# A recurrent unit's last tile in token halves, and the order of the output projection's last products

## The chip, the cores and the metric

The kernel runs on one NeuronCore of a Trainium2 chip, as one program. What counts is the device time of a run in microseconds; the figure of a kernel is the median of its runs. A profiled execution gives the trace; times in it are microseconds from the start of its span. Engines: PE is TensorE (matmuls; its weight loads are PEld), DVE is VectorE, ACT is ScalarE, POOL is GpSimd, and SP mostly issues DMAs.

## The reference, cut to what matters

One inference step of two trunk layers with 1024 features. 512 latent tokens (a grid of 8 rows by 64 columns) and 128 prompt tokens go through layer 0 (attention) and layer 1 (a recurrent unit), each followed by a SwiGLU network. The change lies in layer 1, between its recurrent unit and its output projection:

```python
def _linear_scan(a, b, h0, reverse):
    def step(h, ab):
        a_t, b_t = ab
        h = a_t * h + b_t
        return h, h
...
    b = jnp.sqrt(-jnp.expm1(2.0 * log_a)) * (i * xc)
...
    hs_f, hT_f = _linear_scan(a_f, b_f, h0[:, 0], reverse=False)
    hs_b, hT_b = _linear_scan(a_b, b_b, h0[:, 1], reverse=True)
    y = (hs_f + hs_b).astype(xm.dtype) * jax.nn.gelu(gate)
    return y @ w_out, jnp.stack([hT_f, hT_b], axis=1)
...
        lat = lat + g1_l[:, None, :] * o_l
```

Latent and prompt tokens are scanned apart from each other, each forward and backward; the final states of the prompt scans are an output. All is float32.

## The kernel before, in words

Features lie on the 128 partitions, in eight tiles of 128 (`KT`), tokens along the free axis: columns 0 to 511 latent, 512 to 639 prompt. The two halves of the tokens, `CH`, are columns 0 to 319 and 320 to 639, so the second half holds the last 192 latent columns and all prompt columns. A float32 product is made of three passes: each operand is split into a high part, rounded by a cast to the matmul type (float32r; `whi` or `yhi`), and a low part, the rest (`wlo`, `ylo`); a chunk's 24 matmuls are high x high, high x low and low x high over eight k-tiles. `unit` (L164) loads a weight by SP into one of three `raw` buffers and splits it: cast on ACT, subtraction on DVE (L183). In the recurrent unit's own stage the cast is a DMA of POOL instead (L179).

The recurrent unit is a software pipeline over feature tiles (L1473 to L1487). `lru_a` makes the gates, `lru_b` (L1310) the decay `a` and the input `ti`, whose last two steps are a square root on ACT (L1321) and its product on DVE (L1322) over both directions at once, 2 x 643 columns. `lru_c` (L1325) scans in place on DVE, per direction 512 latent and 128 prompt columns, copies the end states to `st` (L1332), and adds the two directions, the latent ones in two pieces that also turn rows of the grid into columns (L1337), then the prompt ones (L1338). `lru_d` (L1341) multiplies by the gate `G` (L1343) and splits the result into `yhi` (ACT) and `ylo` (DVE); for the last tile it does so in the two token halves. The write of `st` to memory follows on POOL's queue (L1488).

The output projection `project_halves` (L1036) has eight output tiles f. The weights of f = 0 to 2 are ready early. Five chunks, both halves of f = 0 and 1 and the first half of f = 2, are held open in five PSUM banks: three of tag `mm`, two of `mx`, whose third bank is free. They take the k-tiles 0 to 4 in a loop, and the last three k-tiles together, since those come out of the recurrent unit late:

```python
        for k in range(KT - 3, KT):
            if k == KT - 1:
                self.keep(self.ps("at"), 10)
            for (f, t0, t1), ps in turns:
```

`keep` (L207) issues small float32 matmuls that only keep TensorE at work. Ahead of the last k-tile there are ten. When a chunk ends, `out` (L1037) adds it on DVE into `x` (`residual`, L598), squares it on ACT, and writes it to memory by SP. `x` is loaded whole from memory, four DMAs on SP's queue (L1371), into a buffer in the space that the recurrent unit's tiles leave. Then come f = 3 to 7 for the first half, with weights loaded into buffers as they come free, and f = 2 to 7 for the second.

Order: the program is traced in the order of the source, and a scheduler then orders each engine's instructions by its own estimate of the time, so independent work may go ahead of what stands before it. `pin(ins)`, or `issue_after(ins)`, says that an instruction goes behind `ins` on its engine. A tile placed where another lay waits for that one's last reader.

Of the kernel before, what the change touches and what calls it, by code (L numbers as in the profile page):

```python
# [9 lines left out]
F32 = mybir.dt.float32  # L10
F32R = mybir.dt.float32r
AF = mybir.ActivationFunctionType
ALU = mybir.AluOpType
# [4 lines left out]
KT = D // P  # L18
NLAT = 512
NTOK = 640  # L20
# [5 lines left out]
ROWS = 8  # L26
# [8 lines left out]
LW = 643  # L35
NLT = 10
C0 = 515
FG = (1, 1, 1)
MODS = ((0, 2), (0, 4), (0, 3), (0, 5), (1, 1), (1, 0), (1, 4), (1, 3), (1, 2), (1, 5))
# [87 lines left out]
class _Step:  # L127
# [35 lines left out]

    def unit(self, src, slot=None, after=None, nx=3):  # L164
        nc = self.nc
        _, a, b = src.shape
        raw = self.t([P, a, b], F32, "raw", 3)
        nc.sync.dma_start(raw, src)
        if slot is None:
            self.nu += 1  # L170
            slot = "x" if self.wx and self.nu % 2 == 0 else "m"
        if slot == "x":
            hi = self.t([P, a, b], F32R, "whx", nx, self.sb)
            lo = self.t([P, a, b], F32R, "wlx", nx, self.sb)
        else:
            hi = self.t([P, a, b], F32R, "whi", 3)
            lo = self.t([P, a, b], F32R, "wlo", 3)
        if self.ptags == ["at"]:
            nc.gpsimd.dma_start(hi, src)  # L179
        else:  # L180
            nc.scalar.copy(hi, raw)  # L181
        with self.tc.issue_after(after) if after else nullcontext():
            nc.vector.tensor_tensor(lo, raw, hi.bitcast(F32), ALU.subtract)  # L183
        return hi, lo
# [850 lines left out]

    def project_halves(self, w, hi, lo, gk, key, xd):  # L1036
        def out(f, t0, t1, ps):  # L1037
# [6 lines left out]
        for (f, t0, t1), ps in zip(early, pss):  # L1044
            self.some(us[f], hi, lo, t0, t1, ps, range(KT - 3))
        turns = sorted(zip(early, pss), key=lambda e: e[0][1])
        for k in range(KT - 3, KT):
            if k == KT - 1:
                self.keep(self.ps("at"), 10)
            for (f, t0, t1), ps in turns:  # L1050
                for part in us[f]:
                    self.done = self.nc.tensor.matmul(ps, part[:, k], hi[:, k, t0:t1], start=False, stop=False).ins
            for (f, t0, t1), ps in turns:
                self.done = self.nc.tensor.matmul(ps, us[f][0][:, k], lo[:, k, t0:t1], start=False, stop=(k == KT - 1)).ins
                if k == KT - 1:
                    out(f, t0, t1, ps)
        for f in range(3, KT):
            us.append(self.unit(w[f], "mx"[f % 2]))
            out(f, *CH[0], self.chunk(us[f], hi, lo, *CH[0]))
        self.rt = self.t([P, NTOK], F32, "r", 2)  # L1060
# [249 lines left out]
    def lru_b(self, f, lt, tr, ti):  # L1310
# [7 lines left out]
        for d in range(2):  # L1318
            p2 = self.sp2[:, d * KT + f:d * KT + f + 1]
            self.turn(AF.Exp, lambda: nc.scalar.activation(tr[:, d], tr[:, d], AF.Tanh, scale=p2, bias=p2))  # L1320
        self.turn(AF.Sqrt, lambda: nc.scalar.activation(tr, tr, AF.Sqrt, scale=0.25))  # L1321
        nc.vector.tensor_tensor(ti, ti, tr, ALU.mult)  # L1322
        return a, ti

    def lru_c(self, f, a, h):  # L1325
        nc = self.nc
        for d in range(2):
            for sl, init in ((slice(0, NLAT), self.col(f"h{d}", f)), (slice(C0, LW), 0.0)):
                hv, av = [t[:, d, sl] if d == 0 else t[:, d, sl][:, ::-1] for t in (h, a)]
                nc.vector.tensor_tensor_scan(hv, av, hv, init, ALU.mult, ALU.add)  # L1330
        ends = bass.AP(tensor=h.tensor, offset=h[:, 0, LW - 1:LW].offset, ap=[list(h.ap[0]), [C0 + 1, 2]])
        nc.vector.tensor_copy(self.st.rearrange("p (d k) -> p k d", d=2)[:, f], ends)  # L1332
        y = a[:, 0, 0:NTOK]
        fn, bn = [h[:, d, 0:NLAT].rearrange("p (r c) -> p c r", r=ROWS) for d in range(2)]
        for c0, c1, q0 in ((56, 64, 0), (0, 56, 64)):
            yv = y[:, q0:q0 + (c1 - c0) * ROWS].rearrange("p (c r) -> p c r", r=ROWS)
            nc.vector.tensor_tensor(yv, fn[:, c0:c1], bn[:, c0:c1], ALU.add)  # L1337
        nc.vector.tensor_tensor(y[:, NLAT:NTOK], h[:, 0, C0:LW], h[:, 1, C0:LW], ALU.add)  # L1338
        return y

    def lru_d(self, f, y, G, yhi, ylo):  # L1341
        for a, b in CH if f == KT - 1 else ((0, NTOK),):
            self.nc.vector.tensor_tensor(y[:, a:b], y[:, a:b], G[:, a:b], ALU.mult)  # L1343
            self.split(yhi[:, f, a:b], ylo[:, f, a:b], y[:, a:b])

# [27 lines left out]
    def run(self):  # L1373
# [83 lines left out]
        with self.phase("lru", at=1) as lp:  # L1457
# [15 lines left out]
            for t in range(KT + 2):  # L1473
# [5 lines left out]
                if 0 < t <= KT:  # L1479
                    B[t - 1] = self.lru_b(t - 1, *A.pop(t - 1))  # L1480
                if t > 1:
                    C[t - 2] = self.lru_c(t - 2, *B.pop(t - 2))
                for g in {KT - 1: (KT - 3, KT - 2), KT: (KT - 1,)}.get(t, (t - 2,)):
                    for step in gate(g) if 0 < g < KT - 1 + (t == KT) else ():
                        step()
                if t > 1:
                    self.lru_d(t - 2, C.pop(t - 2), G.pop(t - 2), yhi, ylo)  # L1487
            nc.gpsimd.dma_start(o["nh"], self.st)  # L1488
        x1, x2 = self.big(n=PITCH), self.big(n=PITCH)
        self.new_x(self.ctx)  # L1490
        self.load_x(xd)
        with self.phase("ffn1", at=1, mx=3, mc=1, wx=2) as fp:
# [4 lines left out]
            self.X["B12h"], self.X["B12l"] = self.X["T4h"], self.X["T4l"]  # L1497
            self.project_halves(i["wlo"], yhi, ylo, (1, 2), (1, 1), xd)
            self.hhi, self.hlo = self.big(n=PITCH), self.big(n=PITCH)
# [23 lines left out]
```

## Time and profile before

| | us |
|---|---|
| median of 3 runs | 1506.66 |
| lowest and highest | 1506.61, 1507.72 |
| the profiled execution's own time | 1508.43 |
| its span in the trace | 1506.4 |
| PE busy in it | 1483.1 |

The own time of the profiled execution is 2.0 us above its span, for what lies around the span. The trace lists instructions with start and duration. A duration of DVE or ACT holds the way through the engine, so that the next instruction may start a little ahead of its end; where it needs the result it starts behind it. Matmuls overlap likewise: their distance from start to start is the cost. In square brackets stands idle time of the engine ahead of an instruction, and what ended it. Chip time 1003 to 1025 is the stretch around the change.

### The profile page before, as it was taken

How to read it: one execution, taken by the hardware profiler on the slowest of the kernel's cores; microseconds unless marked ns; L12 is line 12 of the kernel's file. 1: busy time of each engine (PE TensorE's matmuls, PEld its weight loads, DVE VectorE, ACT ScalarE, POOL GpSimd, SP SyncE). 2: the span in 40 equal slices, each digit the busy share in tenths (PEclk: the TensorE clock that was granted, in tenths of full speed). 3: DMA queues.
4: the chain of work that ended last, by engine and by line, in shares of the span. 5: the costliest groups of instructions: out<-in, count | busy, mean ns of one | idle time of the engine just before them, and what ended most of it. 6: DMA issues, size and time to landing. Idle time of an engine off the chain costs nothing. (4 is left out here: it accounts for less than half of the span.)

```text
span 1506.4 us, 26172 instructions
## 1 busy us (share of the span) xinstructions
PE 1483.1 (98%) x10409; PEld 1435.1 (95%) x10409; DVE 1063.1 (71%) x2015; ACT 701.6 (47%) x1271; POOL 222.5 (15%) x260
## 2 busy tenths in 40 slices
PE   8999999999999999999999999999999999999997
PEld 6999999899999999999999988899999999999997
DVE  5778998679999997444443778986975665655555
ACT  4576766664332123312321569884634342524243
POOL 0112132101111110000000100000331323232311
PEclk9999999999999999999999999999999999999999
DMA  9644766446566664222222544325233131313221
GB/s 377 174 146 159 188 189 174 119 144 193 182 183 197 208 198 133 62 84 84 65 65 92 148 142 127 106 90 186 103 113 98 57 113 57 112 57 103 66 57 71
DMA packets 72330, 196.66 MB, mean 131 GB/s; under 512 B 8048, under 2 KB 24592, under 8 KB 72080
## 3 DMA queue, kind: packets, MB, share of 16 engines
q1 hardware_dynamic: 57392, 142.32, 29.9%
q0 software_dynamic: 14240, 51.98, 11.4%
q8 instruction: 82, 1.34, 0.4%
q10 hardware_dynamic: 576, 0.68, 0.1%
q14 instruction: 40, 0.33, 0.1%
HBM read 179.48 MB, written 8.92 MB: 125 GB/s over the span
## 5 line engine op out<-in xcount | busy, mean ns | idle before, releaser
L229 PE MATMUL mm<-big,whi 128*128 128x320 f32 (+3 forms) x1224 | 380.3, 311 | 1.1 <-DVE big L1350 0.9
L228 PE MATMUL mm<-big,whi 128*128 128x320 f32 (+3 forms) x1224 | 378.6, 311 | 1.5 <-ACT big L574 0.6
L230 PE MATMUL mm<-big,wlo 128*128 128x320 f32 (+3 forms) x1224 | 378.0, 310 | 0.2 <-DVE wlo L183 0.2
L228 PEld LDWEIGHTS mm<-big,whi 128*128 128x128 f32 x1224 | 229.8, 188 | 3.7 <-ACT big L574 0.9
L229 PEld LDWEIGHTS mm<-big,whi 128*128 128x128 f32 x1224 | 230.1, 188 | 3.2 <-DVE big L1350 1.5
L230 PEld LDWEIGHTS mm<-big,wlo 128*128 128x128 f32 x1224 | 230.5, 188 | 1.6 <-DVE wlo L183 0.5
L257 DVE SCALAR_TENSOR_TENSOR mprod<-mraw,csb 128x1024 f32<-128x1024 f32 x160 | 195.1, 1220 | 11.4 <-DMA mraw<-in_wm 11.0
L598 DVE SCALAR_TENSOR_TENSOR x<-mm,G,x 128x320 f32<-128x320 f32 (+2 forms) x192 | 77.7, 435 | 80.4 <-PE mm L230 80.2
L181 ACT CAST whi<-raw 128x1024 fp32r<-128x1024 f32 (+1 forms) x71 | 73.8, 1040 | 109.5 <-PE mm L229 63.4
L183 DVE TENSOR_TENSOR wlo<-raw,whi 128x1024 fp32r<-128x1024 f32 (+1 forms) x87 | 105.2, 1209 | 24.7 <-ACT whi L181 11.9
L229 PE MATMUL mm<-big,whx 128*128 128x320 f32 (+3 forms) x348 | 108.2, 311 | 0.0
L230 PE MATMUL mm<-big,wlx 128*128 128x320 f32 (+3 forms) x348 | 107.7, 310 | 0.0
L228 PE MATMUL mm<-big,whx 128*128 128x320 f32 (+3 forms) x348 | 107.6, 309 | 0.0
L253 POOL DMA_DIRECT2D mraw<-in_wm x80 | 43.1, 539 | 355.2 <-DVE mprod L257 272.2
L229 PE MATMUL mx<-big,whi 128*128 128x320 f32 (+3 forms) x281 | 87.0, 309 | 0.0
L230 PE MATMUL mx<-big,wlo 128*128 128x320 f32 (+3 forms) x281 | 86.8, 309 | 0.0
L228 PE MATMUL mx<-big,whi 128*128 128x320 f32 (+3 forms) x281 | 86.7, 309 | 0.0
L181 ACT CAST whx<-raw 128x1024 fp32r<-128x1024 f32 (+1 forms) x40 | 41.1, 1029 | 84.6 <-PE mm L229 45.7
L230 PE MATMUL mx<-big,wlx 128*128 128x320 f32 (+3 forms) x260 | 80.5, 309 | 0.0
L229 PE MATMUL mx<-big,whx 128*128 128x320 f32 (+3 forms) x260 | 80.4, 309 | 0.0
L228 PE MATMUL mx<-big,whx 128*128 128x320 f32 (+3 forms) x260 | 80.1, 308 | 0.0
L1348 ACT CAST whi<-raw 128x1024 fp32r<-128x1024 f32 (+1 forms) x41 | 41.3, 1007 | 73.2 <-PE mm L229 44.5
(363 smaller groups left out, 3710.4 us busy)
## 6 DMA issues: line engine op xcount, KB each, us to landing
raw<-in_gu SPq DMA_DIRECT2D x88, 512.0 KB, 3.5
mraw<-in_wm POOLq DMA_DIRECT2D x80, 512.0 KB, 4.0
raw<-in_dn SPq DMA_DIRECT2D x24, 512.0 KB, 3.7
sw<-in_wm SPq DMA_DIRECT2D x16, 512.0 KB, 10.7
raw<-in_wqk SPq DMA_DIRECT2D x16, 512.0 KB, 5.0
raw<-in_wi SPq DMA_DIRECT2D x16, 512.0 KB, 3.5
whi<-in_wi POOLq DMA_DIRECT2D x16, 512.0 KB, 3.9
raw<-in_dn SPq DMA_DIRECT2D x16, 448.0 KB, 3.3
```

The lines of the kernel that those rows point to most:

```text
L181: nc.scalar.copy(hi, raw)
L183: nc.vector.tensor_tensor(lo, raw, hi.bitcast(F32), ALU.subtract)
L228: nc.tensor.matmul(ps, hi[:, k], xhi[:, k, s], start=(k == 0), stop=False)
L229: nc.tensor.matmul(ps, hi[:, k], xlo[:, k, s], start=False, stop=False)
L230: self.done = nc.tensor.matmul(ps, lo[:, k], xhi[:, k, s], start=False, stop=(k == last)).ins
L253: nc.gpsimd.dma_start(w, self.i["wm"][l * 6 + j - 2, f])
L257: nc.vector.scalar_tensor_tensor(prod, w, 1.0, self.csb[:, s], ALU.mult, ALU.mult, accum_out=out[:, s, f:f + 1])
L598: self.nc.vector.scalar_tensor_tensor(xs, ps[:, a - t0:b - t0], G[:, s, f:f + 1], xs, ALU.mult, ALU.add)
L1348: self.nc.scalar.copy(hi, v)
```

## The change

The last tile (f = 7) gets a chain of its own, `lru_end`, in which each DVE instruction is pinned behind the one ahead of it. `lru_b` leaves out its last product for that tile and returns the root instead. The chain makes the latent columns first (root product, one scan per direction, the sum for the columns 0 to 319, gate), then the prompt columns, with the first half's low part between, and copies the states last. In the projection, the last k-tile is taken for the first half's three chunks, then the first half of the fourth output (f = 3) in a bank of `mx`, of which the low x high passes come behind the last k-tile of the second half's two chunks. That output's weight is cast by a DMA of POOL, and its low part is pinned behind the chain's last low part (`ended`), the residuals behind that (`self.low`). Four fillers stand for ten. The write of the states goes behind the projection on POOL's queue. The fifth output's first product is pinned behind the fourth output's last.

```diff
+LATPR = (slice(0, 512), slice(C0, LW))
...
-    def unit(self, src, slot=None, after=None, nx=3):
+    def unit(self, src, slot=None, after=None, nx=3, cast=False):
-        if self.ptags == ["at"]:
+        if cast or self.ptags == ["at"]:
             nc.gpsimd.dma_start(hi, src)
-        with self.tc.issue_after(after) if after else nullcontext():
-            nc.vector.tensor_tensor(lo, raw, hi.bitcast(F32), ALU.subtract)
+        with self.pin(after):
+            self.low = nc.vector.tensor_tensor(lo, raw, hi.bitcast(F32), ALU.subtract).ins
...
         self.halve("T4", k, self.x[:, k + KH, 0:HT])
         self.nc.sync.dma_start(self.x[:, k + KH], xd[(k + KH) * P:(k + KH) * P + P])
 
-    def project_halves(self, w, hi, lo, gk, key, xd):
+    def project_halves(self, w, hi, lo, gk, key, xd, ended):
         def out(f, t0, t1, ps):
             self.residual(f, t0, t1, ps, G, True)
             self.nc.sync.dma_start(xd[f * P:f * P + P, t0:t1], self.x[:, f, t0:t1])
         pss = [(self.ps("mx") if j % 2 else self.pg(False))[:, 0:HT] for j in range(len(early))]
         for (f, t0, t1), ps in zip(early, pss):
             self.some(us[f], hi, lo, t0, t1, ps, range(KT - 3))
-        turns = sorted(zip(early, pss), key=lambda e: e[0][1])
-        for k in range(KT - 3, KT):
-            if k == KT - 1:
-                self.keep(self.ps("at"), 10)
+
+        def turn(k, turns, pin=None):
             for (f, t0, t1), ps in turns:
                 for part in us[f]:
-                    self.done = self.nc.tensor.matmul(ps, part[:, k], hi[:, k, t0:t1], start=False, stop=False).ins
+                    with self.pin(pin):
+                        pin = self.done = self.nc.tensor.matmul(ps, part[:, k], hi[:, k, t0:t1], start=False, stop=False).ins
             for (f, t0, t1), ps in turns:
                 self.done = self.nc.tensor.matmul(ps, us[f][0][:, k], lo[:, k, t0:t1], start=False, stop=(k == KT - 1)).ins
                 if k == KT - 1:
-                    out(f, t0, t1, ps)
-        for f in range(3, KT):
+                    with self.pin(self.low):
+                        out(f, t0, t1, ps)
+        sides = [[e for e in zip(early, pss) if e[0][1:] == c] for c in CH]
+        for k in range(KT - 3, KT - 1):
+            turn(k, sides[0] + sides[1])
+        us.append(self.unit(w[3], "x", ended, cast=True))
+        self.keep(self.ps("at"), 4)
+        turn(KT - 1, sides[0])
+        t0, t1 = CH[0]
+        ps = self.ps("mx")[:, 0:HT]
+        for j, (part, v) in enumerate(((0, hi), (0, lo), (1, hi))):
+            if j == 2:
+                turn(KT - 1, sides[1], self.done)
+            for k in range(KT):
+                self.done = self.nc.tensor.matmul(ps, us[3][part][:, k], v[:, k, t0:t1], start=(j == k == 0),
+                                                  stop=(j == 2 and k == KT - 1)).ins
+        out(3, t0, t1, ps)
+        for f in range(4, KT):
             us.append(self.unit(w[f], "mx"[f % 2]))
-            out(f, *CH[0], self.chunk(us[f], hi, lo, *CH[0]))
+            out(f, *CH[0], self.chunk(us[f], hi, lo, *CH[0], pins={0: self.done} if f == 4 else {}))
         self.rt = self.t([P, NTOK], F32, "r", 2)
         for c, (t0, t1) in enumerate(CH):
             for f in range(KT - DEH, KT) if c else ():
...
             p2 = self.sp2[:, d * KT + f:d * KT + f + 1]
             self.turn(AF.Exp, lambda: nc.scalar.activation(tr[:, d], tr[:, d], AF.Tanh, scale=p2, bias=p2))
         self.turn(AF.Sqrt, lambda: nc.scalar.activation(tr, tr, AF.Sqrt, scale=0.25))
+        if f == KT - 1:
+            return a, ti, tr
         nc.vector.tensor_tensor(ti, ti, tr, ALU.mult)
         return a, ti
 
+    def scan(self, f, a, h, d, part):
+        init = 0.0 if part else self.col(f"h{d}", f)
+        hv, av = [t[:, d, LATPR[part]] if d == 0 else t[:, d, LATPR[part]][:, ::-1] for t in (h, a)]
+        return self.nc.vector.tensor_tensor_scan(hv, av, hv, init, ALU.mult, ALU.add)
+
+    def directions(self, y, h, c0, c1, q0):
+        fn, bn = [h[:, d, 0:NLAT].rearrange("p (r c) -> p c r", r=ROWS) for d in range(2)]
+        yv = y[:, q0:q0 + (c1 - c0) * ROWS].rearrange("p (c r) -> p c r", r=ROWS)
+        return self.nc.vector.tensor_tensor(yv, fn[:, c0:c1], bn[:, c0:c1], ALU.add)
+
+    def states(self, f, h):
+        ends = bass.AP(tensor=h.tensor, offset=h[:, 0, LW - 1:LW].offset, ap=[list(h.ap[0]), [C0 + 1, 2]])
+        return self.nc.vector.tensor_copy(self.st.rearrange("p (d k) -> p k d", d=2)[:, f], ends)
+
     def lru_c(self, f, a, h):
-        nc = self.nc
         for d in range(2):
-            for sl, init in ((slice(0, NLAT), self.col(f"h{d}", f)), (slice(C0, LW), 0.0)):
-                hv, av = [t[:, d, sl] if d == 0 else t[:, d, sl][:, ::-1] for t in (h, a)]
-                nc.vector.tensor_tensor_scan(hv, av, hv, init, ALU.mult, ALU.add)
-        ends = bass.AP(tensor=h.tensor, offset=h[:, 0, LW - 1:LW].offset, ap=[list(h.ap[0]), [C0 + 1, 2]])
-        nc.vector.tensor_copy(self.st.rearrange("p (d k) -> p k d", d=2)[:, f], ends)
+            for part in range(2):
+                self.scan(f, a, h, d, part)
+        self.states(f, h)
         y = a[:, 0, 0:NTOK]
-        fn, bn = [h[:, d, 0:NLAT].rearrange("p (r c) -> p c r", r=ROWS) for d in range(2)]
-        for c0, c1, q0 in ((56, 64, 0), (0, 56, 64)):
-            yv = y[:, q0:q0 + (c1 - c0) * ROWS].rearrange("p (c r) -> p c r", r=ROWS)
-            nc.vector.tensor_tensor(yv, fn[:, c0:c1], bn[:, c0:c1], ALU.add)
-        nc.vector.tensor_tensor(y[:, NLAT:NTOK], h[:, 0, C0:LW], h[:, 1, C0:LW], ALU.add)
+        for piece in ((56, 64, 0), (0, 56, 64)):
+            self.directions(y, h, *piece)
+        self.nc.vector.tensor_tensor(y[:, NLAT:NTOK], h[:, 0, C0:LW], h[:, 1, C0:LW], ALU.add)
         return y
 
     def lru_d(self, f, y, G, yhi, ylo):
-        for a, b in CH if f == KT - 1 else ((0, NTOK),):
-            self.nc.vector.tensor_tensor(y[:, a:b], y[:, a:b], G[:, a:b], ALU.mult)
-            self.split(yhi[:, f, a:b], ylo[:, f, a:b], y[:, a:b])
+        self.nc.vector.tensor_tensor(y, y, G, ALU.mult)
+        self.split(yhi[:, f, 0:NTOK], ylo[:, f, 0:NTOK], y)
+
+    def lru_end(self, f, a, h, root, G, yhi, ylo):
+        nc = self.nc
+        y = a[:, 0, 0:NTOK]
+        ins = None
+
+        def dve(step, *args):
+            nonlocal ins
+            with self.pin(ins):
+                ins = step(*args).ins
+
+        def rooted(part):
+            v = h[:, :, LATPR[part]]
+            dve(nc.vector.tensor_tensor, v, v, root[:, :, LATPR[part]], ALU.mult)
+
+        def gated(t0, t1):
+            dve(nc.vector.tensor_tensor, y[:, t0:t1], y[:, t0:t1], G[:, t0:t1], ALU.mult)
+            nc.scalar.copy(yhi[:, f, t0:t1], y[:, t0:t1])
+
+        def low(t0, t1):
+            dve(nc.vector.tensor_tensor, ylo[:, f, t0:t1], y[:, t0:t1], yhi[:, f, t0:t1].bitcast(F32), ALU.subtract)
+        rooted(0)
+        for d in range(2):
+            dve(self.scan, f, a, h, d, 0)
+        for piece in ((56, 64, 0), (0, 32, 64)):
+            dve(self.directions, y, h, *piece)
+        gated(*CH[0])
+        rooted(1)
+        dve(self.scan, f, a, h, 0, 1)
+        low(*CH[0])
+        dve(self.scan, f, a, h, 1, 1)
+        dve(self.directions, y, h, 32, 56, 320)
+        dve(nc.vector.tensor_tensor, y[:, NLAT:NTOK], h[:, 0, C0:LW], h[:, 1, C0:LW], ALU.add)
+        gated(*CH[1])
+        low(*CH[1])
+        with self.pin(ins):
+            self.states(f, h)
+        return ins
 
     def split(self, hi, lo, v, after=(None, None)):
         with self.pin(after[1]):
...
-                if t > 1:
+                if t > KT:
+                    ended = self.lru_end(t - 2, *B.pop(t - 2), G.pop(t - 2), yhi, ylo)
+                elif t > 1:
-                if t > 1:
+                if 1 < t <= KT:
-            nc.gpsimd.dma_start(o["nh"], self.st)
-            self.project_halves(i["wlo"], yhi, ylo, (1, 2), (1, 1), xd)
+            self.project_halves(i["wlo"], yhi, ylo, (1, 2), (1, 1), xd, ended)
+            nc.gpsimd.dma_start(o["nh"], self.st)
```

## Rows read from the trace of the kernel before

**Rows 1.** The page, busy time of each engine, its share of the span and instructions.

```profile
PE 1483.1 (98%) x10409; PEld 1435.1 (95%) x10409; DVE 1063.1 (71%) x2015; ACT 701.6 (47%) x1271; POOL 222.5 (15%) x260
```

**Rows 2.** The timeline of PE: start, us, engine, line, op, operands, count, [idle<-releaser].

```profile
1006.85 2.39 PE L211 MATMUL at<-ident,ones 128*128 128x128 f32 x20
1010.75 0.42 PE L1052 MATMUL mm<-big,whi 128*128 128x320 f32 x1 [1.51 <-ACT big L1348]
...
1012.33 0.60 PE L1054 MATMUL mm<-big,whi 128*128 128x320 f32 x3
1012.77 0.46 PE L1054 MATMUL mx<-big,whi 128*128 128x320 f32 x2
...
1016.71 0.30 PE L228 MATMUL mm<-big,whi 128*128 128x320 f32 x1
...
1024.01 0.39 PE L230 MATMUL mx<-big,wlo 128*128 128x320 f32 x1
```

**Rows 3.** The timeline of DVE, same columns, from the root product to the seventh output's weights.

```profile
1003.79 1.50 DVE L1322 TENSOR_TENSOR lt<-lt,lt 128x1286 f32<-128x1286 f32 x1 [0.35 <-ACT lt L1321]
1005.32 1.28 DVE L1330 TENSOR_TENSOR_SCAN lt<-lt,cols,lt 128x512 f32<-128x512 f32 x1
1006.52 0.40 DVE L1330 TENSOR_TENSOR_SCAN lt<-lt,lt 128x128 f32<-128x128 f32 x1
1006.84 1.26 DVE L1330 TENSOR_TENSOR_SCAN lt<-lt,cols,lt 128x512 f32<-128x512 f32 x1
...
1008.33 1.21 DVE L1337 TENSOR_TENSOR lt<-lt 128x64 f32<-128x64 f32 x2
...
1009.49 0.32 DVE L1338 TENSOR_TENSOR lt<-lt 128x128 f32<-128x128 f32 x1
1009.69 0.92 DVE L1343 TENSOR_TENSOR lt<-lt,gl 128x320 f32<-128x320 f32 x2
...
1014.71 1.01 DVE L598 SCALAR_TENSOR_TENSOR x<-mm,G,x 128x320 f32<-128x320 f32 x2 [0.26 <-issue]
...
1022.71 1.23 DVE L183 TENSOR_TENSOR wlo<-raw,whi 128x1024 fp32r<-128x1024 f32 x1 [1.45 <-ACT whi L181]
```

**Rows 4.** The timeline of ACT, same columns, in the same stretch.

```profile
1010.24 0.86 ACT L1348 CAST big<-lt 128x320 fp32r<-128x320 f32 x2 [4.43 <-DVE lt L1343]
1011.01 1.99 ACT L181 CAST whx<-raw 128x1024 fp32r<-128x1024 f32 x2
...
1021.63 1.05 ACT L181 CAST whi<-raw 128x1024 fp32r<-128x1024 f32 x1 [1.38 <-DMA raw<-in_wlo]
```

**Rows 5.** The waits of SP's queue, 995 to 1030: total us, times, longest.

```profile
SPq L1371 <- DVE lt L1343: 8.7, 1, 8.7
```

**Rows 6.** The timeline of SP's queue in that stretch, columns as before.

```profile
1010.77 2.13 SPq L1371 DMA_DIRECT2D x<-xd  x4
1013.34 1.48 SPq L168 DMA_DIRECT2D raw<-in_wlo  x2
```

**Rows 7.** Line L1371 alone, its first load of x: us to landing.

```profile
DMA to landing us min/median/max: 3.9/3.9/3.9
```

**Rows 8.** Stretches of 4 us: busy us (instructions) by engine, PEclk, DMA share, GB/s.

```profile
1008.00:1012.00 4.00, 2.49 (x20) 2.30 (x19) 3.51 (x10) 1.76 (x4) 0.56 (x1) 1.00 0.07 13
1012.00:1016.00 4.00, 4.00 (x29) 3.88 (x28) 3.65 (x6) 2.76 (x5) 0.00 (x0) 1.00 0.94 351
```

**Rows 9.** DMA issues, 1000 to 1016: count, KB each, median us to landing.

```profile
raw<-in_wlo SPq DMA_DIRECT2D x3, 512.0 KB, 8.2
```

**Rows 10.** Groups by form, 1003.5 to 1012: busy us, mean ns | idle before.

```profile
L1337 DVE TENSOR_TENSOR lt<-lt 128x448 f32<-128x448 f32 x1 | 1.0, 1027 | 0.0
...
L1337 DVE TENSOR_TENSOR lt<-lt 128x64 f32<-128x64 f32 x1 | 0.3, 260 | 0.0
```

**Rows 11.** The timeline of POOL, 992 to 1028, its only row.

```profile
1009.91 0.56 POOL L1488 DMA_DIRECT2D out_nh<-st  x1 [45.66 <-DVE lt L1338]
```

**Rows 12.** The page's DMA issues: a cast load by POOL, median us to landing.

```profile
whi<-in_wi POOLq DMA_DIRECT2D x16, 512.0 KB, 3.9
```

## The prediction

> **What bounds the kernel now.** I read the page first. TensorE is busy for 1483.1 of 1506.4 us [rows 1], so an edit away from it is worth only what it takes out of a hole in its row. The timeline of PE around the seam between the recurrent unit and its output projection shows that hole [rows 2]: after the products of k-tile 6, twenty filler records (ten calls of `keep`) run from 1006.85 for 2.39 us, then the engine sits idle for 1.51 us until 1010.75, released by ScalarE's cast of the last tile. The hole is 3.90 us, 0.26% of the span, and no speed-up of this chain can win more.
>
> Next the timeline of DVE and of ACT [rows 3, 4] shows the chain that fills the hole: the root product (L1322) starts at 1003.79, as soon as ScalarE's square root is done, then come four scans, the sum of the directions, the copy of the states, the prompt sum, the two gate products (from 1009.69), and the first cast at 1010.24. PE starts 0.51 us after the cast's start.
>
> Last I read what follows the hole, since PE runs there without a pause. The queue of SP had waited 8.7 us for the gate product before the four loads of x [rows 5]: x lies where the recurrent unit kept its gate tiles, and the whole tile waits for their last reader. The loads begin at 1010.77 [rows 6], 0.16 us after the second gate product ends (1009.69 + 0.92 = 1010.61). The first lands 3.9 us later [rows 7], and the first residual (L598) starts at 1014.71, after 0.26 us of idle that is no engine's [rows 3]: that is this landing. From 1012 to 1016 the DMA engines are busy 94% of the time, against 7% in the stretch before [rows 8]. The weights of the seventh output, `w[6]`, are issued at 1013.34 behind these loads [rows 6]; three loads of such weights take 8.2 us in the median here [rows 9]. Their cast waits 1.38 us for the landing and starts at 1021.63 [rows 4], their low part at 1022.71 [rows 3] ends at 1023.94, and PE's third product of that output starts at 1024.01, drawn out to 0.39 us [rows 2]. **So PE meets this weight with no slack at all:** what it wins at the hole, it must wait for there, unless the weight comes earlier too.
>
> **The change, part by part.**
>
> *The first half's chain.* From 1003.79 on: root product on the latent columns only, 1024 elements for 1286. A tensor_tensor of 1024 takes 1.22 (L183, "1022.71 1.23" [rows 3]) for 1.50. Then two scans of 512: the first starts 0.03 after its input, the second 1.20 later (1005.32 to 1006.52) and lasts 1.26 [rows 3], so they end at 1007.50. Sum of the directions: 64 elements take 0.26, 448 take 1.027 [rows 10], so 2.0 ns each between them, and 256 take an estimated 0.64. With 0.18 from the first's start to the second's (the pair's 1.21 [rows 3] less 1.03) they run from 1007.53 to 1008.35. The gate product starts 0.03 after that, lasts an estimated 0.52 (a pair takes 0.92, with starts some 0.40 apart), and the cast starts at 1008.93. PE follows at 1009.44: **1.31 us earlier**. Removed from this path are the two scans of 128 (0.32 each, 1006.52 to 1006.84), 192 columns of the sum, the states and the prompt sum (0.20, 1009.49 to 1009.69); added is what is lost where each step now waits for the one ahead of it.
>
> *The second half's chain.* After the gate (1008.38): root product of 256 (about 0.45), scan of 128 (0.40 [rows 3]), the first half's low part, scan of 128, 192 columns of the sum (0.52), prompt sum (0.32), each pinned to the one ahead. With the overlaps of the rows above where two steps are independent, and 0.03 where one waits, the second gate product runs from 1011.07 to 1011.59, for 1010.61 before: **0.98 us later**. The extra is the low part now ahead of it (0.41), the split root product (0.15), and some 0.45 of waits. Its cast is done by 1012.1 and PE asks for it only after 9 products of the first half and 16 of the fourth output; at 0.146 each (three between 1012.33 and 1012.77 [rows 2]) that is 1013.2. The second half is thus covered with 1.1 us to spare.
>
> *The fourth output's weights.* Its cast leaves ScalarE and becomes a DMA on the queue of POOL, which is idle for 45.66 us before its one write of the states [rows 11]; that write now comes after it and waits for the states, which nothing on the chip waits for. A cast load there lands in 3.9 us [rows 12] and needs a slot that tiles of the recurrent unit held; if these are an earlier tile's, as I take from ScalarE's cast into such a slot, which starts at 1011.01 [rows 4], before the cast pair of the last tile (1010.24 + 0.86) ends that its last low part reads, it can go before 1003 and is there by 1007. Its low part (1.22) is pinned behind the second half's low part, ends at about 1013.7 (or 1015.5, if the sixth output's low part goes first), and PE asks for it at 1014.1. Both are harmless, or hidden by the next wait. The residuals are pinned behind it, and would be waiting for x anyway.
>
> *Fillers.* Four calls for ten: eight records, 0.96 us, ending at 1007.81; they stand in the hole, and PE then idles 1.63 us.
>
> *What the later gate product does.* x is loaded 0.98 us later: issue at 1011.75, first landing at 1015.65, first residual at 1016.2 done. PE has finished the fourth output at 1009.44 + 5.8 = 1015.25 and holds six banks; it can start the next only when the residual frees one. So it starts at 1016.25, for 1016.71 before [rows 2]: 0.85 of the 1.31 us is lost here. The loads of `w[6]` stand behind x on the same queue, in a stretch where the DMA engines have no room (their buffer comes free with the fourth output's low part, at 1013.7 or 1015.5, before the loads of x are through), so they land 0.98 us later as well, and the third product of the seventh output starts at 1024.99 for 1024.01.
>
> **Sum:** -1.31 at the hole, +0.85 at the bank, +1.44 at the weight: **+0.98 us**. From there on PE is as before. The profiled execution took 1508.43 us of its own (span 1506.4), which would be 1509.4; the median of the runs, 1506.66, becomes **1507.6**. That is 0.07%, and what a measurement of this kernel tells from no change is about 0.2%, 3.0 us.
>
> The unseen prices have these ends. The landing of `w[6]`: not later at all (3.9 us as for the first load of x, [rows 7]), or later by x's delay and by one or two of the 160 KB writes of x that could slip ahead of it, 0.47 us each at the 351 GB/s of [rows 8]: 0 to 1.9; I take 0.98, as x stands ahead of it in either. The order of products after the seam is a scheduler's, and anew: I hold it within 1.2 us either way, the size of one 1024-wide step that goes ahead of another on DVE.
>
> **Rivals.**
>
> *The gain stays.* If the scheduler lays another output's second half (its weights are long there) ahead of the seventh output, the wait at the weight is covered, and only the bank is left: -0.46, 1506.2. If x were not later either, it is -1.31, 1505.35. For it: such filling is seen now, since two products of the fifth output (1016.71) stand ahead of the sixth. Against it: at the seventh no such filling stands in the rows though the weight comes to the last 0.1 us. Chance 0.30.
>
> *Slower: the POOL load comes late.* Should its slot be one that the last tile's own buffers held, it waits for the states, behind the second half's low part, at about 1012.7, and then meets the loads of x. It lands 3.9 to 8.2 us later [rows 9, 12], 1016.6 to 1020.9, where PE wants it at 1010.87. With the 1.31 that the seam gave and the rest of the order kept, the next output starts 4.3 to 8.6 us late: 1511.0 to 1515.3. It decides from the point where the load is issued after 1007. The Trainium skill (DMA: Bandwidth & Descriptors, Queues, rings and completion order) says that each DMA engine goes round-robin between the queues that it has work for; by this the load would get half the rate beside x, an estimate nearer to 1016.6 than to 1020.9, and x would lose that share. No row here has two busy queues. For it: the buffers do lie in the same space. Against it: the cast at 1011.01 named above did not wait for the last tile. Chance 0.08.
>
> *The clock falls.* The granted clock is 1.00, the level of 2.4 GHz, in the stretch with the 1.51 us of idle [rows 8]. With fewer fillers the idle time is 1.63 us after 0.96 us of filler. If it fell to 1.2 GHz, the 39 products behind it would take twice 0.146 us: up to +5.7, less the 1.3. The Trainium skill (TensorE: Matmul & The Clock Gate, What's actually happening) says that idle time brings the throttle back, which speaks against taking fillers away; the trace so far does not show it at this length. Chance 0.02.
>
> **How the numbers follow.** Forecast 0.55, gain stays 0.30, POOL late 0.08, clock 0.02, other effects of the new order 0.05. The range is from the end of the second case, 1505.3, to the forecast's upper end: +0.98 + 0.94 for the writes + about half of the 1.2: 1509.2. The two slow rivals beyond it hold 0.10. Faster by over 3 us would need most of the 3.90 us hole and no wait behind: 0.02. Slower by over 3 us: 0.10. Within: 0.88.
>
> **What would show it.** In the changed kernel's timeline: the first product of k-tile 7 about 2.6 us after the fillers' start; loads of x on SP 7.96 us after the start of the root product, for 6.98; an idle PE of about 1 us ahead of the fifth or sixth output; another at the seventh, ended by its low part. The forecast is wrong if x is issued no later than before, if PE shows no idle time at the seventh output, or if the fourth output's first product waits for a DMA.

## The result, and the profile after

The kernel got slower: 1514.36 us in the median of 4 runs (1513.88 to 1515.68) for 1506.68 in the runs of before beside them, a ratio of 1.0048 (95% interval 1.0036 to 1.0061). I had forecast 1507.6, and no change with a chance of 0.88. The profiled execution took 1514.27 us, its span 1512.0. The profiled execution of before was itself 1.8 us above its median, so the two traces differ by 5.6 us only. Absolute times in a trace also move by some 2 us from one execution to the next: the root product starts between 1003.44 (e2, e10) and 1005.58 (e6). Below, stretches are compared by their own windows, or from the start of the root product.

First the seam, in the timeline of PE after the change (start, us, engine, line, operation, operands, count, idle time before and what ended it):

```profile
1009.58 0.41 PE L1052 MATMUL mm<-big,whi 128*128 128x320 f32 x1 [1.07 <-ACT big L1388]
1011.00 2.49 PE L1070 MATMUL mx<-big,whx 128*128 128x320 f32 x16
...
1016.51 0.38 PE L229 MATMUL mm<-big,whx 128*128 128x320 f32 x1 [0.98 <-DVE x L599]
1016.73 0.31 PE L230 MATMUL mm<-big,whx 128*128 128x320 f32 x1
1019.39 0.64 PE L231 MATMUL mm<-big,wlx 128*128 128x320 f32 x1 [2.35 <-DVE wlx L184]
1019.82 0.47 PE L229 MATMUL mm<-big,whx 128*128 128x320 f32 x1
1020.09 0.47 PE L230 MATMUL mm<-big,whx 128*128 128x320 f32 x1
...
1023.05 0.31 PE L230 MATMUL mm<-big,whx 128*128 128x320 f32 x1
...
1028.38 0.30 PE L231 MATMUL mm<-big,wlo 128*128 128x320 f32 x1
```

The last k-tile starts at 1009.58 for 1010.75 [rows 2]: the chain won what it should. The fourth output runs at once behind it (1011.00). Then come two waits. The first, 0.98 us for a residual, is the bank that I had forecast. The second, 2.35 us for a low part, I had not. Behind it the products stand 0.27 us apart (1019.82 to 1020.09) instead of 0.146, until about 1022.7: the granted clock is 0.50 there, the level of 1.2 GHz, for some 13 products, and 1.6 us are lost. The seventh output's product that is the first to read its low part, the third in the source's order, comes at 1028.38 for 1024.01.

What that low part stood behind is seen in the timeline of DVE, same columns:

```profile
1012.72 1.22 DVE L184 TENSOR_TENSOR wlx<-raw,whx 128x1024 fp32r<-128x1024 f32 x1
1015.81 1.01 DVE L599 SCALAR_TENSOR_TENSOR x<-mm,G,x 128x320 f32<-128x320 f32 x2 [1.87 <-DMA x<-xd]
1017.65 0.55 DVE L599 SCALAR_TENSOR_TENSOR x<-mm,G,x 128x320 f32<-128x320 f32 x1 [0.83 <-DMA x<-xd]
1018.12 1.22 DVE L184 TENSOR_TENSOR wlx<-raw,whx 128x1024 fp32r<-128x1024 f32 x1
```

Between the low parts of the fourth output (1012.72) and the sixth (1018.12) stand three residuals, and DVE idles 1.87 and 0.83 us for two loads of x. In the kernel before both low parts stood ahead of the residuals, which began at 1014.71 [rows 3]:

```profile
1012.09 2.36 DVE L183 TENSOR_TENSOR wlx<-raw,whx 128x1024 fp32r<-128x1024 f32 x2 [0.46 <-ACT whx L181]
```

The same happened on ScalarE. This is its timeline:

```profile
1012.12 1.04 ACT L182 CAST whx<-raw 128x1024 fp32r<-128x1024 f32 x1
1016.44 0.47 ACT L533 ACTIVATE ssq<-x 128x320 f32<-128x320 f32 x1 [3.29 <-DVE x L599]
...
1018.24 0.47 ACT L536 ACTIVATE sq<-x 128x320 f32<-128x320 f32 x1 [0.91 <-DVE x L599]
1018.61 1.03 ACT L182 CAST whi<-raw 128x1024 fp32r<-128x1024 f32 x1
```

The sixth output's cast was done by 1013.16, so its low part could have begun at 1013.94, where the fourth's ends. The fifth output's cast (1018.61) stands behind squares that wait for the residuals; before, the casts ran from 1011.01 on [rows 4], and the fifth output's stood ahead of all squares too:

```profile
1013.11 1.05 ACT L181 CAST whi<-raw 128x1024 fp32r<-128x1024 f32 x1
1015.30 0.47 ACT L532 ACTIVATE ssq<-x 128x320 f32<-128x320 f32 x1 [1.13 <-DVE x L598]
```

Work that waits for x had moved ahead of work that does not.

The second loss lies 40 us later, at the second half's moment: the small matmuls (L552, L555) that sum the squares of x over the partitions, for the normalisation of the next stage. PE's timeline ahead of it:

```profile
1057.88 0.31 PE L231 MATMUL mm<-big,wlx 128*128 128x320 f32 x1
1060.84 0.77 PE L552 MATMUL at<-ones,ssq 128*128 128x128 f32 x2 [2.64 <-DVE ssq L538]
1061.40 0.63 PE L555 MATMUL at<-ones,sq 128*128 128x128 f32 x2
```

The moment waits 2.64 us for a sum of squares. Before, the 24 products of the first gate chunk of the next stage (L1168 to L1170) stood there, from 1053.93 to the moment at 1057.44, and filled the wait:

```profile
1053.93 0.31 PE L1168 MATMUL mm<-big,whx 128*128 128x320 f32 x1
...
1057.44 0.38 PE L551 MATMUL at<-ones,ssq 128*128 128x128 f32 x2
```

Now they come after it, from 1066.56. The windows of both kernels say it all in two lines each; first before, then after (us, then busy us and instructions of PE, PEld, DVE, ACT and POOL, granted clock, DMA share, GB/s):

```profile
1016.00:1022.00 6.00, 6.00 (x43) 6.00 (x43) 5.12 (x12) 2.42 (x6) 0.00 (x0) 1.00 0.99 334
1056.00:1062.00 6.00, 5.73 (x43) 5.50 (x43) 4.30 (x7) 2.88 (x4) 0.85 (x1) 1.00 0.58 203
```

```profile
1016.00:1022.00 6.00, 3.14 (x12) 2.91 (x13) 5.07 (x11) 2.28 (x4) 0.00 (x0) 0.78 0.99 335
1056.00:1062.00 6.00, 3.36 (x20) 3.12 (x20) 5.10 (x12) 3.44 (x8) 0.00 (x0) 0.86 0.40 140
```

Twice PE loses nearly half of a 6 us stretch, and each time the granted clock falls besides.

### The profile page after: what moved, and what is told of

It reads as the page before. It is cut to its first block, busy times and chain, and to the rows that moved or that the text cites. A ratio compares the mean times of both kernels' runs of the same rounds, so it can differ in the third digit from the quotient of the medians.

```text
span 1512.0 us, 26157 instructions
## 1 busy us (share of the span) xinstructions
PE 1484.9 (98%) x10397; PEld 1436.4 (95%) x10397; DVE 1060.8 (70%) x2017; ACT 700.1 (46%) x1270; POOL 224.7 (15%) x261
## 5 line engine op out<-in xcount | busy, mean ns | idle before, releaser
L599 DVE SCALAR_TENSOR_TENSOR x<-mm,G,x 128x128 f32<-128x128 f32 (+2 forms) x193 | 77.7, 434 | 82.1 <-PE mm L231 79.4
L229 PE MATMUL mm<-big,whx 128*128 128x320 f32 (+3 forms) x352 | 109.4, 311 | 1.0 <-DVE x L599 1.0
L230 PE MATMUL mm<-big,whx 128*128 128x320 f32 (+3 forms) x352 | 109.9, 312 | 0.0
L230 PE MATMUL mx<-big,whx 128*128 128x320 f32 (+3 forms) x248 | 76.8, 310 | 0.0
L231 PE MATMUL mx<-big,wlx 128*128 128x320 f32 (+3 forms) x248 | 76.8, 310 | 0.0
L229 PE MATMUL mx<-big,whx 128*128 128x320 f32 (+3 forms) x248 | 76.6, 309 | 0.0
```

What stands on the lines that cost most here:

```text
L229: nc.tensor.matmul(ps, hi[:, k], xhi[:, k, s], start=(k == 0), stop=False)
L230: nc.tensor.matmul(ps, hi[:, k], xlo[:, k, s], start=False, stop=False)
L231: self.done = nc.tensor.matmul(ps, lo[:, k], xhi[:, k, s], start=False, stop=(k == last)).ins
L599: self.nc.vector.scalar_tensor_tensor(xs, ps[:, a - t0:b - t0], G[:, s, f:f + 1], xs, ALU.mult, ALU.add)
```

## Experiments

The theory: two separate losses, both made by the order and not by the chain. **Queue**: DVE, ACT and PE take their instructions in order, and work that needs only a weight now stands behind work that needs x. **Count**: the fourth output's bank is taken by `ps`, which does not move the counter `ng` (L148), so every later chunk gets the kind of bank (`mm` or `mx`) that the chunk ahead of it would have had, and with it another place in PE's order. The rivals: x comes too late whatever the order, or one of the two losses is all of it.

**e1: the sixth output's low part ahead of the residuals**

```diff
         us.append(self.unit(w[3], "x", ended, cast=True))
+        u5 = self.unit(w[5], "x", self.low)
...
-            us.append(self.unit(w[f], "mx"[f % 2]))
+            us.append(u5 if f == 5 else self.unit(w[f], "mx"[f % 2]))
```

> One edit to the changed kernel: the sixth output's weight is taken up right behind the fourth's, so that its low part stands on DVE ahead of the early residuals. Theory A (the order on DVE): PE's 2.35 us wait for that low part behind the sixth output's second product goes, and with it the stretch of granted clock 0.50 up to 1022.70 (some 13 products at 0.267 for 0.146, 1.5 us): the seventh output's third product then waits for its own weight alone and comes near 1025.0 for 1028.38, the first spread near 1042.7 for 1046.08, the time 1511.0 to 1511.6 for 1514.4. Theory B (the count of PSUM banks costs it all, later): unchanged within 0.7 us. Theory C (the later load of x and of the last two weights): PE stops as long as before in the same stretch, for x or for a weight, and the time stays within 1 us.

Measured: 1515.9 us, ratio to before 1.0053 (1.0040 to 1.0066). No gain: a miss. The profiled execution took 1519.34, 3.4 us above the median, and its root product starts 1.41 us later than in the changed kernel. PE's timeline:

```profile
1018.00 0.39 PE L229 MATMUL mm<-big,whx 128*128 128x320 f32 x1 [1.01 <-DVE x L599]
...
1025.99 0.64 PE L229 MATMUL mm<-big,whi 128*128 128x320 f32 x1 [3.54 <-ACT whi L182]
1026.42 0.47 PE L230 MATMUL mm<-big,whi 128*128 128x320 f32 x1
...
1026.96 0.47 PE L231 MATMUL mx<-big,wlo 128*128 128x320 f32 x1
```

The 2.35 us are gone, and a wait of 3.54 us stands in their place, for the cast of the seventh output (`w[6]`). That PE stops as long for another weight is the sign that the expectation gave to its theory C. The cast waits for its load and starts 19.65 us after the root product, for 19.69 in the changed kernel and 17.84 before, so this weight was as late in the changed kernel, hidden behind the other wait. It costs more than it need: the 22 products of the fifth output that are left (`mx`, from 1026.96) use a weight that is ready, but stand behind the seventh's first two in PE's order. Before, they stood ahead and covered that wait, as its timeline shows from 1020.51 on; the seventh output follows there with its third product at 1024.01 [rows 2]:

```profile
1020.51 0.30 PE L230 MATMUL mm<-big,wlo 128*128 128x320 f32 x1
1020.65 0.30 PE L228 MATMUL mm<-big,whi 128*128 128x320 f32 x1
```

In e1 the clock falls again, to 0.50 from 1026 to 1032. One wait taken out of a row of in-order waits only shows the next.

**e2: the bank counted**

```diff
-        ps = self.ps("mx")[:, 0:HT]
+        ps = self.pg()[:, 0:HT]
```

> One edit to the changed kernel: the fourth output's bank is taken through the helper that counts the banks, as the kernel before did; it still gets an mx bank. Theory B: all later products get the bank kinds of the kernel before, the first gate product of the next stage again stands ahead of the second moment, PE's 2.64 us wait at 1060.84 goes, and the time falls by 2 to 3.5 us, to 1511 to 1512.4; the 2.35 us wait near 1017 stays. Theory A alone: the products ahead of the second moment are only done later, and the time stays within 0.7 us of 1514.4.

Measured: 1510.97 us, ratio 1.0022 (1.0013 to 1.0030), just under the range of theory B. Its windows:

```profile
1016.00:1022.00 6.00, 2.81 (x14) 2.82 (x15) 5.34 (x11) 2.28 (x4) 0.00 (x0) 0.86 1.01 352
...
1056.00:1062.00 6.00, 6.00 (x44) 6.00 (x43) 5.36 (x11) 4.90 (x10) 0.00 (x0) 1.00 0.16 56
```

The second loss is gone, PE is busy throughout, the clock stays. The first loss is as large as in the changed kernel (42.15 us from the root product to the first half's spread, L569, the matmuls that spread the normalisation factor over the partitions, for 42.25, and 37.89 before), but in another dress: the 2.35 us that I expected to stay are gone, and the fifth output now stands first in PE's order and waits 4.03 us for its cast.

```profile
1019.18 0.41 PE L229 MATMUL mm<-big,whi 128*128 128x320 f32 x1 [4.03 <-ACT whi L182]
```

**e3: e1 and e2 together**

> Both edits together. If A and B hold and add up, the two stalls go and what is left is what the prediction worked out: the hole's gain less the bank and the seventh output's weight, 1507 to 1508.5 us, same as before within 0.1%. If the loss lies in the later transfers (theory C), it stays above 1511.

Measured: 1510.79 us, ratio 1.0022 (1.0013 to 1.0031), as e2 alone, and not what I expected. The sixth output's low part is early now, but the wait for the fifth output's cast is 3.90 us.

**e0: the kernel before once more**

> The kernel before once more, for a second profiled execution. If the first one (1508.43 for a median of 1506.7) was disturbed by chance, this one lies within 0.5 us of the median, the PE waits of 1.46 us near 1093 and 1.0 us near 1102 are gone or shorter, and the trace of after then stands some 7 us behind it by the end. If it is how the kernel runs under the profiler, it comes out near 1508.4 again.

Measured: 1507.28 us, span 1505.2, between the two cases; the root product starts at 1003.75 and the first spread (L568) at 1042.11 for 1041.68. The seam is the same but for 0.47 us: here PE waits 0.29 us for the seventh output's low part, which came just in time in the first trace. The wait of 1.46 us near 1093 comes again, as 1.40. I draw no more from it.

**e4: the changed chain with the projection of before** (`project_halves` as it was)

```diff
-        def turn(k, turns, pin=None):
...
+        turns = sorted(zip(early, pss), key=lambda e: e[0][1])
+        for k in range(KT - 3, KT):
...
```

> The changed chain of the recurrent unit with the projection of the kernel before. Theory P (the loss comes from the projection's new order: the count of the banks, and the casts and low parts of the fifth and sixth outputs' weights queued behind the residuals and squares that wait for x): low parts of the fourth and sixth outputs stand ahead of the residuals again, the first plain product ahead of the second moment, and the kernel lies where the prediction's own sum puts it or lower, 1506.0 to 1508.0. Theory X (the chain's second half delays the load of x by 1 us and that is what costs): it stays above 1510.

Measured: 1508.94 us, ratio 1.0010 (1.0001 to 1.0018), 0.9 us above the expected range. Some four fifths of the loss are gone while x is as late as in the changed kernel (its loads go 8.04 us after the root product, for 8.05): the loss needs the projection's order, and the late load alone does not make it. The edit undoes order and count together, so it does not part Queue from Count.

**e5: e2, and the fifth output's weight early, its low part first**

```diff
         us.append(self.unit(w[3], "x", ended, cast=True))
+        us.append(self.unit(w[4], "x", self.low))
...
-            us.append(self.unit(w[f], "mx"[f % 2]))
+            if f > 4:
+                us.append(self.unit(w[f], "xm"[f % 2]))
```

> The changed kernel with the banks counted, the fifth output's weight (in place of the sixth's) in the buffers that are free early, and its low part ahead of the residuals; x is loaded as late as before. Theory P: the 3.9 us wait for the fifth output's cast (seen with the banks counted) goes, PE waits about 1 us for the first residual and then, since everything behind still follows x, some 1 to 3 us for the sixth output's low part or the seventh's cast; 1507.5 to 1509.5 in all. Theory X: x itself is the bound, and nothing under 1510 is reached.

Measured: 1513.30 us, ratio 1.0038 (1.0025 to 1.0050): a miss; by its number alone it is what theory X gives, which e4 excludes. The fifth output no longer waits, but the sixth's cast (`whi`) was now put on ACT behind the seventh's (`whx`), which waits for its load, and PE idles 4.27 us for it:

```profile
1024.29 1.04 ACT L182 CAST whx<-raw 128x1024 fp32r<-128x1024 f32 x1 [4.08 <-DMA raw<-in_wlo]
1025.24 1.04 ACT L182 CAST whi<-raw 128x1024 fp32r<-128x1024 f32 x1
```

**e6: e2, and x loaded early.** The last gate tile goes into a spare buffer of the recurrent unit that x does not cover, so x's loads no longer wait for the chain.

```diff
-        G = self.t([P, NTOK], F32, "gl", 3, lp)
+        G = self.t([P, 2, LW], F32, "lt", NLT, lp)[:, 0, 0:NTOK] if f == KT - 1 else self.t([P, NTOK], F32, "gl", 3, lp)
```

> The changed kernel with the banks counted and the last gate tile in a spare buffer outside x, so that x can be loaded while the chain runs (near 1003 instead of 1011.9); order on DVE and ACT as in the changed kernel. Theory P: the residuals run at once behind the fourth output's low part (near 1014), the fifth output's cast comes near 1016 instead of 1018.1, and PE waits 1 to 1.5 us for it instead of 4.0; the seventh output's weight lands without x beside it, and no clock falls: 3 us less than the kernel with only the banks counted (1510.97), 1506.5 to 1508.0. If x is not what the queue behind the residuals waits for, the 4.0 us stay and the time is 1510 to 1511.

Measured: 1506.53 us, ratio 0.9994 (0.9986 to 1.0003). PE's timeline:

```profile
1011.32 0.41 PE L1052 MATMUL mm<-big,whi 128*128 128x320 f32 x1 [0.94 <-ACT big L1388]
...
1018.56 0.41 PE L229 MATMUL mm<-big,whi 128*128 128x320 f32 x1 [1.29 <-ACT whi L182]
```

The order on DVE and ACT is the same as in e2, but what stands at the head of the queues no longer waits for x: PE waits 1.29 us for 4.03.

**e7: e5 and e6 together**

> All of it: banks counted, x early, the fifth output's weight early and its low part ahead of the residuals. Theory P: nothing is left between the chain and the moment, the 1.2 us that the chain wins at the last k tile stay: 1505.0 to 1506.2, faster than both. If a wait that the other stalls hid comes up (the sixth output's cast, near 1017 to 1019), it lands at 1506.5 to 1508.

Measured: 1505.45 us, ratio 0.9988 (0.9979 to 0.9997): some 1.8 us under the kernel before, by an interval that ends just below 1, and far under the changed one. Behind the seam's first product PE has no wait left up to the second moment. Its windows:

```profile
1016.00:1022.00 6.00, 5.89 (x38) 5.63 (x39) 5.71 (x12) 4.79 (x8) 0.00 (x0) 1.00 0.86 298
...
1056.00:1062.00 6.00, 5.94 (x45) 5.71 (x44) 4.27 (x6) 2.54 (x4) 0.85 (x1) 1.00 0.69 220
```

**e8: the changed projection behind the chain of before**

```diff
-                    ended = self.lru_end(t - 2, *B.pop(t - 2), G.pop(t - 2), yhi, ylo)
...
+                    ended = self.lru_d(t - 2, C.pop(t - 2), G.pop(t - 2), yhi, ylo)
```

> The projection of the changed kernel behind the chain of the kernel before (the chain's whole layout undone, the projection's order kept). Theory P (the projection's order costs: casts and low parts queued behind work that waits for x, and banks not counted): the whole loss is there without the chain's new layout, and the chain's win at the last k tile is missing besides: 1514 to 1517. If the loss needs the chain's new layout, it falls to within 1.5 us of before, under 1508.5.

Measured: 1515.77 us, ratio 1.0054 (1.0041 to 1.0067). A loss as large is there without the chain's new layout. The wait at the second moment is the same (2.56 us), but at the seam neither the 0.98 nor the 2.35 us appears. PE waits 2.43 us for the fourth output's load instead, behind which the clock falls too, so the run does not show what the projection's order costs there by itself. That load's timeline on POOL is:

```profile
1010.11 0.55 POOL L1562 DMA_DIRECT2D out_nh<-st  x1 [45.63 <-DVE lt L1363]
1010.65 0.54 POOL L180 DMA_DIRECT2D whx<-in_wlo  x1
```

Here the load stands behind the write of the states, which waits for the chain. That is my rival of the late POOL load, and as the rows read its cause is a place in a queue; no run moves the write alone. In the changed kernel the load went at 998.63, long ahead of the write.

**e9: x early alone** (the edit of e6, banks uncounted)

> The changed kernel with the last gate tile outside x and nothing else, so x is loaded early and the banks stay uncounted. Theory P: the waits of 0.98 and 2.35 us near 1017 and the fallen clock behind them go or shrink to under 1 us; the 2.64 us wait at the second moment stays. Counting alone saved 3.4 us and x early 4.4 us on top of it; if they add, 1509.5 to 1511.0. If the counting only helps where x is early, or the other way, it is outside that.

Measured: 1509.65 us, ratio 1.0019 (1.0010 to 1.0027). At the seam 0.68 us of waiting is left; the wait at the second moment stays (2.66 us). Its windows:

```profile
1016.00:1022.00 6.00, 5.32 (x37) 5.06 (x36) 5.90 (x11) 3.39 (x6) 0.00 (x0) 1.00 0.97 309
...
1056.00:1062.00 6.00, 4.91 (x25) 4.94 (x26) 4.51 (x6) 1.07 (x4) 0.85 (x1) 0.72 0.46 153
```

So x early takes away the forecast wait for the bank with the other, and the two losses are separate, and they add: from +0.48% counting takes 0.26 (e2), x early 0.29 (e9), both 0.54 (e6), where 0.55 is their sum.

**e10: the kernel before with x early**

> The kernel before with the last gate tile outside x. Theory P says that x is not what the kernel before waits for (its weights' casts and low parts stand ahead of the residuals, and PE has no wait for a bank), so the time stays within 0.1% of before: 1505.5 to 1507.5. If x's load bounded the kernel before as well, it gains 2 us or more and the new order had no part in the loss.

Measured: 1507.18 us, ratio 0.9997 (0.9988 to 1.0006). So PE of the kernel before did not wait for x.

**e11: e4 with x early**

> The changed chain with the projection of the kernel before and x early. Chain alone gave 1508.94 with waits of 0.69 us for the fourth output's low part and 0.69 us for the seventh's. With x early the seventh's goes, since its weight lands without x beside it: 1507.5 to 1508.5 by medians of that run; the wait for the chain's second half (1.09 us) and the fourth's low part stay.

Measured: 1508.40 us, ratio 1.0006 (0.9997 to 1.0014). The time is as expected, the waits are so in part: those of 0.69 us for the fourth and the seventh output's low parts are both gone, where I had expected the fourth's to stay; those for the chain's second half (1.11 us) and at the second spread (0.62) stay.

## Why the prediction was wrong

*The first half's chain: right.* Forecast -1.31, measured -1.17 (-1.21 from the root product). The root product took 1.23 us for 1.22, and the cast came at 1009.06 for a forecast of 1008.93.

*The later load of x and the bank: right.* The loads went at 1011.88 (forecast 1011.75), the first residual began at 1015.81 (1015.65), and PE waited 0.98 us and began at 1016.51 (1016.25).

*The fourth output's weights and the second half's chain: right.* The POOL load went at 998.63, PE never waited for it, and the second half's first product came at 1013.32 without a wait.

*The seventh output's weight: not reached.* Its cast came at 1023.52, 1.89 us later than before where I had 0.98, but PE was later still; no idle time at the seventh output was one of the prediction's own signs of being wrong. That PE met this weight without slack before hung on filling that I had not seen: "at the seventh no such filling stands in the rows" holds for [rows 2] only, and the trace has 22 products of the fifth output there, from 1020.51 on.

**The step that failed** is the last of the sum: "The order of products after the seam is a scheduler's, and anew: I hold it within 1.2 us either way, the size of one 1024-wide step that goes ahead of another on DVE." An instruction placed ahead of another costs not its own length but what it waits for. The sixth output's low part was ready to run at 1013.94 and began at 1018.12, 4.2 us later, because three residuals waited for x ahead of it. I had asked only whether the sixth's low part goes ahead of the fourth's, not what happens if it goes behind the residuals. The pin that the change puts on these residuals names the fourth output's low part, and nothing in it holds the sixth's; why the scheduler then put it last is not shown. Where the term allowed 1.2 us, the wait of 2.35 us and the 1.6 us at the lower clock behind it make 3.95. x early wins back some 0.29% (e9), 4.4 us, which also holds most of the 0.98 us at the bank that the sum already had.

**The second step that failed** is one that is missing. I counted the banks only to the fifth output ("holds six banks") and wrote that "from there on PE is as before". The counter moves on with every chunk, and one call that passes it by changed the banks of the next stage; 0.26%, 3.9 us, hung on that (e2). Why the scheduler places a chunk in the other bank behind the moment was not settled; that the count decides it is shown.

*The clock.* I gave 0.02 to a fall at the fillers, and there it held: 1.00 with 1.07 us of idle. It fell at both new waits, which I had not forecast. The Trainium skill (TensorE: Matmul & The Clock Gate, What's actually happening) says that idle time brings the throttle back; the trace agrees at both places, with 0.78 and 0.86 in the windows above.

*The sum itself* comes near the chain alone (e4) only by luck: that run gave +0.10% (0.01 to 0.18), 1.5 us, where I had +0.98, but its waits are others: 0.34 and 1.09 us for the chain's two casts, 0.69 each for two low parts.

## What to carry to other kernels

When an edit re-orders a seam, list for each in-order queue what will stand ahead of what, and price a swap by the wait of the instruction in front, not by its length. Keep work that needs only a weight ahead of work that needs a late transfer; pin both, or bring the transfer forward, as moving one gate tile out of its way did here. A helper that counts (banks, buffers) must be called as often as before, or the next stage is laid out anew.

## What was not expected of the hardware

The clock's fall at short waits. PE's clock stayed at 1.00 through waits of 1.51 us (before), 1.29 us (e6) and 0.98 us, and was at 0.50 at once behind waits of 2.35 us (with 0.98 us just ahead), 2.64 us (the moment) and 3.54 us (e1). That cost some 1.6, 1.3 and 2.8 us on top of the waits: in e1 the 22 products from 1026.96 stand 0.255 us apart in the mean, for 0.146. The length of the wait alone does not tell when it falls: behind 4.03 us (e2) the first 8 products still ran at the full rate and some 12 after them at 0.267 us, and behind 2.51 us (the moment of e1) the 12 small matmuls of the moment ran at the full rate and 13 products after them did not.

The same rows can run at another clock. From 11.90 to 25.23 us the changed kernel and e1 have the same rows of PE at the same times to 0.01 us, with the same waits of 0.30, 0.20 and 0.17 us. These are their windows behind it, the changed kernel first:

```profile
24.00:30.00 6.00, 5.62 (x48) 3.85 (x40) 6.00 (x9) 1.79 (x2) 0.00 (x0) 1.00 1.03 410
```

```profile
24.00:30.00 6.00, 5.62 (x40) 3.56 (x32) 6.00 (x9) 1.79 (x2) 0.00 (x0) 0.72 1.02 408
```

In e1 the granted clock is 0.72 in that window, and eight products fewer are through by its end; from there on e1 is later, and its root product starts at 1005.24 for 1003.83. e3, e4, e5 and e6 have 0.72 there too, the other nine executions 1.00. Ahead of 11.90 us the waits differ (0.54 and 0.82 us in e1 for 0.28 and 0.55), but PE's busy time from 6 to 12 us does not sort them: e7 has 4.25 us and keeps its clock, e3 has 4.86 and loses it. The cause was not found. It is a reason to compare stretches by their own start, and it hides a difference of a microsecond between single executions.
